# w_down: the column groups back and forth over the chunks, stored sums copied into the banks of a group's last run, low parts by DMA in two runs

## The chip, the cores and the metric

The kernel runs on one core of a Trainium2 chip. The time is that of the device for one execution, in microseconds; the median of several executions counts.

## The reference

One layer of an encoder with 512 tokens, a model width of 2048 and a hidden width of 5632, in float32: a projection, two kinds of attention side by side, an output projection with residual, and a SwiGLU block, with a final norm. The change touches only the last product of the SwiGLU block.

```python
h = rmsnorm(x, ffn_norm_w[l])
x = x + (jax.nn.silu(h @ w_gate[l]) * (h @ w_up[l])) @ w_down[l]
return rmsnorm(x, final_norm_w)
```

## The kernel before

**Precision.** The matmuls take operands in a shorter format (fp32r), and every operand is split in two: a high part, the number cast to that format by ACT, and a low part, the rest, by a subtraction on DVE. A product is three matmuls: high by high, high by low, low by high.

**Seven products in place of eight.** In the gate and up products and in `w_down`, the work is done in blocks of two by two, with seven products of sums of blocks in place of eight. `Blocks` holds what both share. An item is one load of weights `raw` (512 KB, R), a tile `S` of sums made from it (`sums`: three instructions of DVE, L1130 to L1132), and the splits (`split`: two casts of ACT, L1142, 128x768 for R and 128x1024 for S; and two subtractions of DVE, L1147). Every tile of that size lies in one of the slots `b` (s4); results and operands of 128x512 lie in the slots `a` (s2). A slot goes back to the end of the list of free ones when the last instruction that uses it is written, and the next `get` takes it from the front; with a kind given, it takes the first free slot that was used for that kind last. A slot's next writer waits until its last reader has ended. `most` is the number of raw loads that may be ahead.

**w_down.** Four jobs do k-tiles 0 to 3 and add their result to the residual in DRAM (`xd`). Then `Down.run` does the k-tiles 4 to 35, which are 16 pairs q = 2 to 17 of k-tiles, for each of four column groups c of 512 columns: 64 items. An item is 42 matmuls of 128x256 (`products`, L1539 to L1541), seven products of six, one PSUM bank for each of the seven. The pairs are cut in three chunks X (2 to 7), Y (8 to 12) and Z (13 to 17), and the order is chunk by chunk, in a chunk column group by column group, so there are 12 runs over the same c. At the end of each run the seven banks are copied out by ACT (`evac`, L1556 and L1558): four right after their products, three ("late") behind the splits of the next item. They go to `md` in DRAM, plain on SP's queue in the first chunk, adding on POOL's queue (GpSimd's DMAs) in the other two. After a group's last run `combine` reads its seven sums back (L1579), forms the four result tiles on DVE (L1590, L1591) and adds them, scaled, to the residual (L1604). It is a generator in `urgent`, of which one step is taken after each item.

**The operands.** For each q, `operands` makes four activation tiles and splits them (DVE L1488 to L1491, ACT L1500 and L1503, DVE L1501 and L1504), from `gd` in DRAM. `make(1)` takes one of the three steps of a q, after the products, where c is 3 or the item's number is odd; and as many as are missing when an item's q is not made yet. A q's slots are given back in c = 3.

**Around it.** The program writes instructions in the order of the Python code; each engine executes its own in that order, and waits are set by the tiles. After `Down` come the jobs for k-tiles 36 to 39 ("later", L303 to L305 and the splits L201, L202), then the last four k-tiles, the residual (L1419) and the final norm. An item's loop is in `run`: load, sums of up to two items ahead, splits of this and the next item, late evacuations, operands, products, one step of `urgent`.

## Time and profile before

| | |
|---|---|
| median of 3 executions | 2208.02 us (2207.67 to 2209.81) |
| the profiled execution | 2210.67 us, span 2208.9 us |
| mean granted TensorE clock | 0.997 |
| `Down` (64 items) | 1773.67 to 2106.80 us of the span |
| behind it, up to the last k-tiles | 2106.80 to 2166.00 us |
| last k-tiles and final norm | 2166.00 to 2208.90 us |

PE is TensorE's matmuls, PEld its weight loads, DVE VectorE, ACT ScalarE, POOL GpSimd, SP the engine that issues most DMAs. In the code, `R` and `S` are `b` slots, `pu` are PSUM banks in this stage. PEclk is the granted clock, 1.00 the full one. In the rows of waits, the first name is the engine, tile and line that waited, the second what ended the wait. In a timeline, the first two numbers are the start and the time of a row, and the bracket holds the idle time ahead of it and what ended it.

### The profile page before, as it was taken

Reading aid. Unit: us, or ns where it says so; the run is one execution under the profiler, and the core shown is the slowest. Engines: PE = TensorE matmul, PEld = TensorE weight load, DVE = VectorE, ACT = ScalarE, POOL = GpSimd, SP = SyncE. Lnnn points to the kernel's source line nnn. Section 1 sums busy time; section 2 is a strip of 40 time slices with the busy share of each in tenths; the row PEclk is TensorE's granted clock in tenths of the full one; section 3 lists DMA queues with packets and bytes.
Section 4 is the critical chain, followed back from the end, with each engine's and each line's share of the span. In section 5 each row is a group of like instructions: output and inputs, shape, how many; then the busy total and the mean of one; then the engine's idle time right before and its main releaser. Section 6 shows DMA issues by size and latency. Waiting matters only on the chain.

```text
span 2208.9 us, 33105 instructions
## 1 busy us (share of the span) xinstructions
PE 2185.1 (99%) x12374; PEld 1909.9 (86%) x12374; DVE 1564.8 (71%) x2720; ACT 1189.8 (54%) x1990; POOL 326.3 (15%) x349
## 2 busy tenths in 40 slices
PE   9999999999999999999999999999999999999998
PEld 7888888888888888888888888888888899999976
DVE  4366665754455346888888888888888897878777
ACT  5344444444445346666666666666666655555442
POOL 0000000000000011222222222222222200122220
PEclk9999999999999999999999999999999999999999
DMA  6525625241324434888888888888989865687892
GB/s 208 160 72 151 176 83 141 84 134 58 96 67 166 139 105 113 193 193 204 204 206 201 201 207 193 208 204 196 211 194 215 247 185 182 184 190 187 225 364 77
DMA packets 260273, 376.75 MB, mean 171 GB/s; under 512 B 18287, under 2 KB 179743, under 8 KB 260112
## 3 DMA queue, kind: packets, MB, share of 16 engines
q1 hardware_dynamic: 192800, 259.37, 37.3%
q0 software_dynamic: 66128, 114.21, 27.6%
q8 instruction: 97, 1.59, 0.3%
q10 hardware_dynamic: 1184, 1.06, 0.1%
q14 instruction: 64, 0.52, 0.1%
HBM read 246.58 MB, written 46.20 MB: 133 GB/s over the span
## 4 chain that ended last, share of the span: by engine, by line
PE 90%; DVE 4%; DMA 4%; ACT 1%; issue 1%; SPq 0%; ACTq 0%; DVEq 0%
PE pd L1275 22%; PE pd L1281 11%; PE ps L303 5%; PE ps L305 5%; PE ps L304 5%; PE ps L295 5%; PE ps L297 5%; PE ps L296 5%; PE pe L1275 4%; PE pu L1541 3%; PE pu L1540 3%; PE pu L1539 3%; PE pe L1281 2%; DMA b<-in_w_down_dram 2%; PE ps L529 1%; DVE b L1147 1%
## 5 line engine op out<-in xcount | busy, mean ns | idle before, releaser
L1275 PE MATMUL pd<-a,b 128*128 128x512 f32 x2112 | 528.4, 392 | 0.1
L1275 PEld LDWEIGHTS pd<-a,b 128*128 128x128 f32 x2112 | 378.9, 188 | 66.3 <-DVE a L1036 0.5
L1281 PEld LDWEIGHTS pd<-a,b 128*128 128x128 f32 x2112 | 288.5, 190 | 21.6
L1281 PE MATMUL pd<-a,b 128*128 128x256 f32 x2112 | 294.9, 282 | 0.0
L202 DVE TENSOR_TENSOR a<-b,a 128x512 fp32r<-128x512 f32 x288 | 192.9, 686 | 137.6 <-ACT a L201 136.2
L1182 POOL DMA_DIRECT2D b<-b x176 | 209.8, 1248 | 521.7 <-ACT b L1181 393.7
L1220 ACT CAST b<-b 128x1024 fp32r<-128x1024 f32 x176 | 185.4, 1053 | 166.6 <-DVE b L1206 138.4
L1541 PE MATMUL pu<-b,a 128*128 128x256 f32 x896 | 255.4, 285 | 6.4 <-DVE a L1504 5.4
L1540 PE MATMUL pu<-b,a 128*128 128x256 f32 x896 | 254.9, 285 | 0.0
L1539 PE MATMUL pu<-b,a 128*128 128x256 f32 x896 | 254.9, 284 | 0.0
L1221 DVE TENSOR_TENSOR b<-b,b 128x1024 fp32r<-128x1024 f32 x176 | 214.8, 1221 | 50.7 <-ACT b L1220 26.3
L201 ACT CAST a<-b 128x512 fp32r<-128x512 f32 x288 | 169.7, 617 | 68.1 <-PE ps L305 22.3
L1541 PEld LDWEIGHTS pu<-b,a 128*128 128x128 f32 x896 | 173.4, 194 | 7.2 <-DVE a L1504 6.1
L1539 PEld LDWEIGHTS pu<-b,a 128*128 128x128 f32 x896 | 173.5, 194 | 0.0
L1540 PEld LDWEIGHTS pu<-b,a 128*128 128x128 f32 x896 | 173.4, 194 | 0.0
L1142 ACT CAST b<-b 128x768 fp32r<-128x768 f32 (+1 forms) x128 | 115.2, 946 | 86.2 <-PE pu L1541 31.0
L1303 DVE TENSOR_TENSOR a<-pd,a 128x512 f32<-128x512 f32 x132 | 91.4, 692 | 96.5 <-ACT a L1302 96.5
L1181 ACT ACTIVATE b<-b 128x768 fp32r<-128x768 f32 x176 | 149.2, 847 | 4.7 <-PE ps L305 2.9
L1147 DVE TENSOR_TENSOR b<-b,b 128x768 fp32r<-128x768 f32 (+1 forms) x128 | 134.5, 1086 | 22.0 <-ACT b L1142 21.9
L1183 ACT CAST b<-b 128x768 fp32r<-128x768 f32 x176 | 145.2, 825 | 0.6 <-PE ps L305 0.6
L1302 ACT COPY a<-pd 128x512 f32<-128x512 f32 x132 | 77.5, 587 | 103.2 <-PE pd L1281 103.2
L1203 DVE TENSOR_TENSOR b<-b 128x512 f32<-128x512 f32 x176 | 120.3, 684 | 0.0
(246 smaller groups left out, 4328.8 us busy)
## 6 DMA issues: line engine op xcount, KB each, us to landing
b<-b POOLq DMA_DIRECT2D x176, 384.0 KB, 5.3
b<-in_w_gate_dram SPq DMA_DIRECT2D x88, 512.0 KB, 4.0
b<-in_w_up_dram SPq DMA_DIRECT2D x88, 512.0 KB, 4.5
b<-in_w_down_dram SPq DMA_DIRECT2D x88, 512.0 KB, 5.5
b<-in_w_in_dram SPq DMA_DIRECT2D x48, 512.0 KB, 4.0
b<-in_w_in_dram SPq DMA_DIRECT2D x94, 256.0 KB, 4.3
b<-in_w_out_dram SPq DMA_DIRECT2D x32, 512.0 KB, 4.7
md<-a POOLq DMA_DIRECT2D x56, 256.0 KB, 8.1
```

The costliest lines, as they stand in the source:

```text
L201: act.copy(h[2].t, r)
L202: dve.tensor_tensor(h[3].t, r, h[2].f, op=OP.subtract)
L1147: dve.tensor_tensor(lo.t, src, hi.f, op=OP.subtract)
L1181: act.activation(lo.t, r, AF.Copy, scale=-1.0)
L1182: pool.dma_start(out=lo.f, in_=r, accum_op=OP.add)
L1220: act.copy(hi.t, self.S[i].t)
L1221: dve.tensor_tensor(lo.t, self.S[i].t, hi.f, op=OP.subtract)
L1275: mm(o, wh.t[:, p, k], x_.t.rearrange("p s t -> p (s t)"), start=first and p == 0, stop=False, skip_group_check=True)
L1281: mm(o[:, 256:512], wl.t[:, p, k], x_.t[:, 0], start=False, stop=last and p == 1, skip_group_check=True)
L1539: mm(o, xh[:, t], wh, start=first and h == 0, stop=False, skip_group_check=True)
L1540: mm(o, xh[:, t], wl, start=False, stop=False, skip_group_check=True)
L1541: mm(o, xl[:, t], wh, start=False, stop=last, skip_group_check=True)
```

## The change

- **Order.** Ten runs in place of 12: groups 0, 1, 2 over X, group 3 over X and Y, groups 2 and 1 over Y, group 0 over Y and Z, groups 1, 2 and 3 over Z. They are numbered 0 to 9 here. The first six evacuate all seven banks at once, on POOL's queue.
- **Stored sums into banks.** Runs 6 to 9 are a group's last. One item ahead of such a run its seven sums are fetched from `md` (`fetch`), and in the last item of the run before, ACT copies them into the banks that come free (`preload`, L1564), in turn with the evacuations (L1609) or with the combine. The run then adds its products to them.
- **Combine from the banks.** In the last item of runs 6 to 9, `combine(c, n, bank)` follows each product: ACT copies two banks (L1627, L1635), DVE does seven operations (L1621, L1622, L1638), and the residual's four (L1652) come in two steps of `urgent`.
- **Low parts by DMA.** In runs 3 and 6 (21 items) the low part of R is made by an activation of ACT with scale −1 (L1481) and an adding DMA on POOL's queue (L1482) in place of DVE's subtraction.
- **Slots and operands.** `S`, splits and parts name a kind of slot; `most` goes from 3 to 4; `make` stands ahead of the products, takes one step more in runs 3 and 6, and keeps more slots back in runs 4 and 5.

```diff
-                S = self.S[i] = s4.get(F32, self.shape(4))
+                S = self.S[i] = s4.get(F32, self.shape(4), "sum")
...
-                    hi = s4.get(F32R, shape)
+                    hi = s4.get(F32R, shape, "split")
...
+                self.runs = [(0, X), (1, X), (2, X), (3, X + Y), (2, Y), (1, Y), (0, Y + Z), (1, Z), (2, Z), (3, Z)]
+                self.reserve = self.most = 4
...
+            def summed(self, r):
+                return r >= 6
+
+            def by_dma(self, i):
+                return i < self.n and self.seq[i][0] in (3, 6)
+
+            def part(self, i):
+                if not self.by_dma(i) or i in self.parts or i in self.sets:
+                    return
+                if i not in self.raw:
+                    self.load()
+                r = self.raw[i].t[:, :, 1:4]
+                hi, lo = (s4.get(F32R, self.shape(3), "part") for _ in range(2))
+                act.activation(lo.t, r, AF.Copy, scale=-1.0)
+                pool.dma_start(out=lo.f, in_=r, accum_op=OP.add)
+                act.copy(hi.t, r)
+                self.parts[i] = (hi, lo)
...
-                    if not raws or len(s2.free) < 9 + 4:
+                    if not raws or len(s2.free) < 9 + self.reserve:
...
+            def fetch(self, r):
+                c = self.runs[r][0]
+                for n in range(7):
+                    self.m[n] = s2.get()
+                    sp.dma_start(out=self.m[n].t, in_=md[7 * c + n])
+
+            def preload(self, n):
+                b = ps.get()
+                act.copy(b.t, self.m[n].t)
+                put(self.m.pop(n))
+                self.pre.append(b)
...
+                if ahead:
+                    self.preload(0)
...
-                        mm(o, xh[:, t], wh, start=first and h == 0, stop=False, skip_group_check=True)
+                        mm(o, xh[:, t], wh, start=first and not loaded and h == 0, stop=False, skip_group_check=True)
...
                     if last:
-                        if n < 4:
-                            self.evac(ch, c, n, self.banks[n])
+                        if loaded:
+                            self.combine(c, n, self.banks[n])
                         else:
-                            self.late.append((ch, c, n, self.banks[n]))
+                            self.evac(c, n, self.banks[n])
+                        if ahead and n < 6:
+                            self.preload(n + 1)
...
+                if n == 0:
+                    self.v, self.y = s2.get(), []
+                    act.copy(self.v.t, bank.t)
+                elif n == 1:
+                    self.y.append(s4.get(F32, [P, 2, 512]))
+                    add(self.y[0].t[:, :, up], M, halves(self.v))
+                elif n == 2:
+                    sub(self.v.t, self.v.t, bank.t)
+                elif n == 3:
+                    self.m4, self.w = s2.get(), s2.get()
+                    act.copy(self.m4.t, bank.t)
+                    add(self.w.t, self.m4.t, self.v.t)
+                elif n == 4:
+                    dve.scalar_tensor_tensor(self.v.t, bank.t, -1.0, self.v.t, op0=OP.mult, op1=OP.subtract)
+                elif n == 5:
+                    self.y.append(s4.get(F32, [P, 2, 512]))
+                    add(self.y[1].t[:, :, up], M, halves(self.w))
+                    sub(self.y[1].t[:, :, lo], halves(self.v), halves(self.m4))
+                    put(self.w, self.m4)
+                else:
+                    sub(self.y[0].t[:, :, lo], halves(self.v), M)
+                    put(self.v)
+                    urgent.append(self.residuals(c, self.y))
+                put(bank)
...
                     self.split(i + 1)
-                    self.evac_late()
+                    self.part(i + 2)
+                    self.reserve = 11 if r in (4, 5) else 4
                     while q not in self.x:
+                        self.reserve = 0
                         self.make(1)
+                    self.make((r in (3, 6)) + i % 2)
+                    if n == len(part) - 2 and r + 1 < len(self.runs) and self.summed(r + 1):
+                        self.fetch(r + 1)
...
                     self.products(i)
-                    if c == 3 or i % 2:
-                        self.make(1)
```

**The order at three places.** A name such as b12_1565 is slot b12 and a number that counts the tiles; the row says the output first, then what is read.

ACT, the casts for items 31 to 34, which lie within a run in both orders. Before (rows of the operands between the second and the third pair are left out; the raw tile is read first, then S):

```order
L1142 CAST b12_1565_18857<-b15_1548_18610 128x768
L1142 CAST b18_1566_18859<-b5_1557_18768 128x1024
L1142 CAST b10_1571_18913<-b6_1556_18702 128x768
L1142 CAST b1_1572_18915<-b9_1564_18853 128x1024
...
L1142 CAST b2_1577_18973<-b13_1562_18780 128x768
L1142 CAST b4_1578_18975<-b11_1570_18909 128x1024
L1142 CAST b12_1583_19029<-b15_1569_18865 128x768
L1142 CAST b19_1584_19031<-b5_1576_18969 128x1024
```

And after the change:

```order
L1142 CAST b3_1566_18846<-b1_1545_18574 128x768
L1142 CAST b12_1567_18848<-b17_1559_18779 128x1024
L1142 CAST b4_1572_18902<-b13_1551_18635 128x768
L1142 CAST b0_1573_18904<-b18_1565_18842 128x1024
L1142 CAST b3_1578_18958<-b15_1558_18710 128x768
L1142 CAST b5_1579_18960<-b17_1571_18898 128x1024
L1142 CAST b4_1584_19014<-b6_1564_18791 128x768
L1142 CAST b2_1585_19016<-b18_1577_18954 128x1024
```

The output slots of the casts of R were b12, b10, b2, b12, and are now b3, b4, b3, b4.

DVE, the operands of q = 11 and 12, whose first items are 27 and 28. Before: the subtraction of item 28's splits, q = 11's last four rows, then item 29's subtraction (L1147) and q = 12's last two behind the left-out rows:

```order
L1147 TENSOR_TENSOR b19_1547_18608<-b10_1537_18542,b18_1545_18604 128x1024
L1501 SCALAR_TENSOR_TENSOR a0_1348_18612<-b17_1499_18143,a0_1348_18612 128x256
L1504 TENSOR_TENSOR a58_1350_18614<-b17_1499_18143,a35_1349_18613 128x512
L1504 TENSOR_TENSOR a20_1352_18616<-a43_1346_18536,a4_1351_18615 128x512
L1504 TENSOR_TENSOR a46_1354_18618<-a37_1347_18537,a61_1353_18617 128x512
...
L1147 TENSOR_TENSOR b17_1555_18700<-b14_1543_18598,b1_1553_18696 128x1024
L1504 TENSOR_TENSOR a33_1361_18681<-a19_1355_18629,a32_1360_18680 128x512
L1504 TENSOR_TENSOR a52_1363_18683<-a24_1356_18630,a12_1362_18682 128x512
```

After the change: the subtraction for item 25 (L1494 is L1147's place for items with a low part by DMA), the last two rows of q = 11, the subtractions for items 26 and 27, and the last two of q = 12:

```order
L1494 TENSOR_TENSOR b4_1531_18434<-b17_1522_18353,b12_1530_18433 128x1024
L1538 TENSOR_TENSOR a31_1345_18378<-a15_1339_18368,a18_1344_18377 128x512
L1538 TENSOR_TENSOR a46_1347_18380<-a51_1340_18369,a43_1346_18379 128x512
...
L1494 TENSOR_TENSOR b3_1537_18495<-b18_1529_18429,b2_1536_18494 128x1024
...
L1494 TENSOR_TENSOR b12_1544_18571<-b17_1535_18490,b5_1543_18570 128x1024
L1538 TENSOR_TENSOR a20_1354_18515<-a42_1348_18505,a4_1353_18514 128x512
L1538 TENSOR_TENSOR a24_1356_18517<-a37_1349_18506,a61_1355_18516 128x512
```

q = 11 was finished behind item 28's subtraction and is now finished behind item 25's; q = 12 was finished behind item 29's and is now finished behind item 27's.

DVE, the combine. Before: the first steps of a group's combine, one step of two operations to an item (the rows that are left out are two of the sums):

```order
L1147 TENSOR_TENSOR b3_1713_20443<-b15_1697_20258,b4_1711_20439 128x768
L1147 TENSOR_TENSOR b18_1714_20445<-b10_1704_20362,b0_1712_20441 128x1024
L1590 TENSOR_TENSOR b12_1716_20507<-a53_1445_20178,a46_1444_20177 128x2x256
L1591 TENSOR_TENSOR a57_1446_20179<-a46_1444_20177,a57_1446_20179 128x512
L1130 TENSOR_TENSOR b19_1718_20511<-b13_1709_20374 128x512
...
L1147 TENSOR_TENSOR b14_1721_20519<-b6_1703_20316,b11_1719_20515 128x768
L1147 TENSOR_TENSOR b7_1722_20521<-b8_1710_20435,b9_1720_20517 128x1024
L1591 TENSOR_TENSOR a13_1448_20181<-a13_1448_20181,a57_1446_20179 128x512
L1590 TENSOR_TENSOR a57_1446_20179<-a54_1447_20180,a57_1446_20179 128x512
```

After the change: the last item of run 6, with the subtractions of the next item, the seven operations of the combine, two residuals, and then the next sums:

```order
L1147 TENSOR_TENSOR b5_1678_20055<-b15_1656_19793,b3_1676_20051 128x768
L1147 TENSOR_TENSOR b9_1679_20057<-b17_1671_19981,b12_1677_20053 128x1024
L1621 TENSOR_TENSOR b2_1681_20079<-pu3_60_19363,a18_1441_20069 128x2x256
L1622 TENSOR_TENSOR a18_1441_20069<-a18_1441_20069,pu4_61_19374 128x512
L1621 TENSOR_TENSOR a43_1443_20099<-a31_1442_20098,a18_1441_20069 128x512
L1638 SCALAR_TENSOR_TENSOR a18_1441_20069<-pu6_63_19396,a18_1441_20069 128x512
L1621 TENSOR_TENSOR b10_1682_20119<-pu7_64_19407,a43_1443_20099 128x2x256
L1622 TENSOR_TENSOR b10_1682_20119<-a18_1441_20069,a31_1442_20098 128x2x256
L1622 TENSOR_TENSOR b2_1681_20079<-a18_1441_20069,pu0_65_19418 128x2x256
L1652 SCALAR_TENSOR_TENSOR a37_1403_19524<-b2_1681_20079,small_76,a37_1403_19524 128x512
L1652 SCALAR_TENSOR_TENSOR a1_1404_19525<-b2_1681_20079,small_76,a1_1404_19525 128x512
L1130 TENSOR_TENSOR b17_1683_20133<-b1_1668_19928 128x512
```

The operations of a combine stood in pairs between the work of one item and the next, and now all seven and two residuals stand between the subtractions of one item and the sums ahead of those of the next.

More of the change, by code (lines that the diff above doesn't have):

```diff
@@ L1451, in layer, with __init__ @@
         class Down(Blocks):
-            def __init__(self, chunks):
-                self.chunks = chunks
-                self.begin([(ch, c, q) for ch in range(len(chunks)) for c in range(4) for q in chunks[ch]], 1, 256)
-                self.x = {}
-                self.making = self.operands()
-                self.late = []
-            def source(self, ch, c, q):
-                return w_down, 2 * q, 2, c * 512, 512
+            def __init__(self, X, Y, Z):
+                self.runs = [(0, X), (1, X), (2, X), (3, X + Y), (2, Y), (1, Y), (0, Y + Z), (1, Z), (2, Z), (3, Z)]
+                self.pairs = X + Y + Z
+                self.drop = {q: r for r, part in ((3, X), (6, Y), (9, Z)) for q in part}
+                self.begin([(r, q) for r, (c, part) in enumerate(self.runs) for q in part], 1, 256)
+                self.x, self.parts, self.m, self.pre, self.seen = {}, {}, {}, [], set()
+                self.reserve = self.most = 4
+                self.making = self.operands()
@@ new lines, in source @@
+            def source(self, r, q):
+                return w_down, 2 * q, 2, self.runs[r][0] * 512, 512
+            def summed(self, r):
[13 more added lines that the diff above has]
+                self.parts[i] = (hi, lo)
@@ new lines, in split @@
+            def split(self, i):
+                if not self.by_dma(i):
+                    return super().split(i)
+                if i in self.sets:
+                    return
+                self.part(i)
+                hi, lo = (s4.get(F32R, self.shape(4), "split") for _ in range(2))
+                act.copy(hi.t, self.S[i].t)
+                dve.tensor_tensor(lo.t, self.S[i].t, hi.f, op=OP.subtract)
+                self.sets[i] = [self.parts.pop(i), (hi, lo)]
+                put(self.raw.pop(i), self.S.pop(i))
+                self.load()
@@ L1525, in products @@
                 Z = lambda n: (sh.t[:, 0, n], sl.t[:, 0, n])
-                first, last = q == self.chunks[ch][0], q == self.chunks[ch][-1]
+                first, last = q == part[0], q == part[-1]
+                ahead = last and r + 1 < len(self.runs) and self.summed(r + 1)
                 if first:
-                    self.banks = []
+                    self.banks, self.pre = self.pre, []
+                loaded = self.summed(r)
+                if ahead:
+                    self.preload(0)
                 x_ = self.x[q]
@@ L1532, in products @@
                 for n, ((wh, wl), x) in enumerate(prods):
-                    if first:
+                    if first and not loaded:
                         self.banks.append(ps.get())
@@ L1559, in evac @@
                 put(bank)
[L1560 removed]
+                if (c, n) in self.seen:
                     pool.dma_start(out=md[7 * c + n], in_=y.t, accum_op=OP.add)
                 else:
[L1563 removed]
+                    pool.dma_start(out=md[7 * c + n], in_=y.t)
+                self.seen.add((c, n))
                 put(y)
[L1566 to L1571 removed]
@@ L1573, in combine @@
[L1573 to L1588 removed]
+            def combine(self, c, n, bank):
@@ L1610, in run @@
             def run(self):
-                for i, (ch, c, q) in enumerate(self.seq):
+                for i, (r, q) in enumerate(self.seq):
+                    c, part = self.runs[r]
+                    n = part.index(q)
                     self.load()
```

64 lines of the change are left out of this document (16 added, 48 removed).

## The prediction

> **What bounds the kernel now.** I read the first page for shares, then busy times by stage for w_down, then what TensorE waited for, then single rows round each gap.
>
> ```profile
> span 2208.9 us, 33105 instructions
> PE 2185.1 (99%) x12374; PEld 1909.9 (86%) x12374; DVE 1564.8 (71%) x2720; ACT 1189.8 (54%) x1990; POOL 326.3 (15%) x349
> ```
>
> TensorE is the bound. The change leaves its matmuls alone, so only TensorE's gaps and its clock can move the time. By stage (us, then busy time of PE, PEld, DVE, ACT, POOL, then PEclk, DMA share, GB/s):
>
> ```profile
> 1773.67:1909.74 136.07, 136.07 (x1135) 136.07 (x1134) 112.24 (x174) 75.67 (x109) 2.72 (x4) 1.00 0.59 185
> 1909.74:1924.94 15.20, 12.34 (x87) 11.73 (x85) 14.91 (x27) 7.60 (x12) 3.69 (x5) 0.89 0.74 186
> 1924.94:2020.69 95.75, 95.75 (x800) 95.75 (x799) 78.30 (x125) 54.70 (x80) 20.84 (x24) 1.00 0.80 190
> 2020.69:2031.04 10.35, 6.78 (x45) 6.58 (x44) 8.45 (x14) 5.16 (x9) 3.47 (x5) 0.84 0.73 123
> 2031.04:2106.80 75.76, 75.76 (x633) 75.76 (x632) 54.06 (x78) 36.76 (x52) 20.50 (x27) 1.00 0.91 249
> 2106.80:2166.00 59.20, 55.58 (x237) 43.75 (x237) 51.21 (x82) 22.03 (x38) 11.42 (x20) 1.00 0.82 283
> 2166.00:2208.90 42.90, 33.60 (x149) 27.37 (x147) 29.04 (x62) 14.19 (x42) 0.00 (x0) 0.95 0.27 98
> ```
>
> Rows 1, 3 and 5 hold 27, 19 and 15 items of `Down` without a gap: 136.07 / 27 = 95.75 / 19 = 5.04 us an item, 0.12 us a matmul. Rows 2 and 4 hold items 27, 28 and 48: 25.55 us where three items take 15.13, so **10.4 us** are lost there. What ended TensorE's waits (sum, count, longest), in `Down` and behind it:
>
> ```profile
> PE pu L1541 <- DVE a L1504: 5.4, 2, 3.6
> PE pu L1541 <- DVE a L1501: 0.9, 1, 0.9
> ...
> PE pu L303 <- DVE a L1419: 1.6, 1, 1.6
> PE pu L1720 <- DVE b L202: 1.0, 2, 0.9
> ```
>
> In `Down` it is the operands of q = 11, 12 and 17, which `make` finishes only when their first item is due (L1501, L1504). The other 4.1 us, 10.4 less 6.3, are half clock and shorter steps:
>
> ```profile
> 1919.99 0.39 PE L1541 MATMUL pu<-b,a 128*128 128x256 f32 x1 [1.83 <-DVE a L1504]
> 2026.10 0.38 PE L1541 MATMUL pu<-b,a 128*128 128x256 f32 x1 [3.57 <-DVE a L1504]
> 2142.93 0.47 PE L303 MATMUL pu<-a,a 128*128 128x512 f32 x1 [1.64 <-DVE a L1419]
> ...
> 1917.71:1921.12 3.41, 1.57 (x13) 1.37 (x13) 3.38 (x7) 1.05 (x3) 1.75 (x2) 1.00 0.73 162
> 1921.12:1924.53 3.41, 3.41 (x18) 3.41 (x18) 3.26 (x6) 3.11 (x6) 1.72 (x2) 0.50 1.05 180
> 2139.56:2142.97 3.41, 1.77 (x9) 1.18 (x7) 3.41 (x7) 2.42 (x6) 0.26 (x1) 1.00 1.04 411
> 2142.97:2146.38 3.41, 3.41 (x15) 2.85 (x16) 3.41 (x6) 2.70 (x5) 0.00 (x0) 1.00 1.05 409
> ```
>
> The first window has a gap of 1.83 us and the 3.41 us behind it run at clock 0.50, which costs about 3.41 / 2, less what falls on waits: 1.5 us. A gap of 1.64 us left the next window at 1.00. So here the line lies between 1.64 and 1.83 us.
>
> **The change part by part.**
>
> *Operand waits.* In the new order q = 12's operands are finished two items before item 28 and q = 17's two before item 48; nothing is forced there. The 10.4 us go: **−10.4** (bounds −10.4 and, if half the clock loss comes back elsewhere, −8.4).
>
> *Lead of the splits.* Before, the casts of an item stand two items ahead of it:
>
> ```profile
> 1940.30 1.79 ACT L1142 CAST b<-b 128x768 fp32r<-128x768 f32 x2 [3.25 <-PE pu L1541]
> 1946.01 2.75 ACT L1558 COPY a<-pu 128x512 f32<-128x512 f32 x4 [3.93 <-PE pu L1541]
> 1896.35 1.07 ACT L1558 COPY a<-pu 128x512 f32<-128x512 f32 x2
> ```
>
> The row at 1940.30 is the cast of item 34, which starts at 1950.13 (1924.94 + 5 x 5.04): 9.8 us ahead. In the new order the kind "split" hands the same two sets of slots back and forth (b3, b4, b3, b4 in place of b12, b10, b2, b12), and a set is free only when the item two earlier has ended. So a cast can start 4.8 us ahead, not 9.8. In a plain item that costs nothing: cast and subtraction of both parts end within 3.2 us. At the run ends, where other work stands ahead of the casts, the cover is gone. The rates:
>
> ```profile
> L1142 ACT CAST b<-b 128x1024 fp32r<-128x1024 f32 x63 | 66.3, 1052 | 5.0 <-DVE b L1132 5.0
> L1142 ACT CAST b<-b 128x768 fp32r<-128x768 f32 x63 | 52.9, 840 | 81.1 <-PE pu L1541 31.0 <-issue 23.7 <-PE pu L1540 16.0
> L1147 DVE TENSOR_TENSOR b<-b,b 128x1024 fp32r<-128x1024 f32 x63 | 76.8, 1219 | 0.0
> L1147 DVE TENSOR_TENSOR b<-b,b 128x768 fp32r<-128x768 f32 x63 | 60.0, 952 | 22.0 <-ACT b L1142 21.9
> L1558 ACT COPY a<-pu 128x512 f32<-128x512 f32 x72 | 41.4, 590 | 52.3 <-PE pu L1541 47.9
> 2057.72 0.68 DVE L1590 TENSOR_TENSOR b<-a,a 128x512 f32<-128x512 f32 x1
> 2058.32 0.68 DVE L1591 TENSOR_TENSOR a<-a,a 128x512 f32<-128x512 f32 x1
> 2058.92 0.68 DVE L1130 TENSOR_TENSOR b<-b 128x512 f32<-128x512 f32 x1
> ...
> 2060.44 2.08 DVE L1147 TENSOR_TENSOR b<-b,b 128x768 fp32r<-128x768 f32 x2
> 2079.50 1.41 DVE L1604 SCALAR_TENSOR_TENSOR a<-b,small,a 128x512 f32<-128x512 f32 x2
> ```
>
> So a 128x512 operation of DVE takes 0.60 us from start to start, the three sums 1.52 (2058.92 to 2060.44), both subtractions about 2.1, two residuals 1.4; ACT copies a bank in about 0.6. A bank as the source of DVE isn't in these rows for TENSOR_TENSOR; I take 0.60, and 0.70 as the upper bound.
>
> *Run ends 0 to 4.* Seven evacuations at once in place of four and three: ACT has 7 x 0.59 = 4.1 us of copies in an item of 5.04 us and casts 0.5 us later. That is under the 1.6 us left (4.8 less 3.2), so **0** (0 to +2).
>
> *Run end 5 to 6.* ACT alternates seven preloads and seven evacuations, each waiting for the bank that the other frees: some 1.0 to 1.15 us a pair, so ACT comes free at T + 9.5 to 10.5 (T: TensorE's start of the run's last item). Queued behind are the cast of the sums for the item that starts at T + 10.1 and the low part of the item after. I reckon 1.2 us of stall for each and take **+2.5** (bounds 1.5 and 4).
>
> *Run ends 6 to 7, 7 to 8, 8 to 9.* This is the dear part. DVE has the next item's subtractions until T + 3.2. Then the combine, interleaved with ACT's copies, since a preload needs the bank that a combine step frees: two steps end at T + 4.4, ACT's third and fourth preloads and the copy of M4 at T + 5.6, then five DVE steps end at T + 8.75. Two residuals (1.4) and three sums (1.5) stand ahead of the subtraction for the item that starts at T + 10.1, and that (0.95) ends at T + 12.7. TensorE needs it at T + 10.2: a stall of 2.5 us. At 6 to 7 the order starts earlier and I get 1.8. Together **+7.0**. From below: if the combine's DVE steps ran as early as the banks are done (the last at T + 5.04, one step to T + 5.7), the subtraction would end at T + 9.6 and nothing stall: 0. From above, with 0.70 for each of seven steps: 3 x 0.7 more, 9.
>
> *Clock.* Two of those gaps, 2.5 us, lie above the 1.83 that halved the clock, though the gap must also lie well in a window. At 0.7 each, 2 x 0.7 x 1.5 = **+2.1** (0 to 4.5). The Trainium skill, "TensorE: Matmul & The Clock Gate", in its rules for kernels, asks only that gaps stay under about 3 us, and puts the half clock behind a whole idle window; by it gaps of 2.5 us cost no clock and the sum would be 2.1 lower. The rows above show a halved window behind 1.83 us, so I go by them.
>
> *Low parts by DMA in runs 3 and 6.* 21 subtractions of 128x768 (0.95 us) leave DVE, which has slack there; 21 activations join ACT, and 21 accumulating transfers of 384 KB POOL's queue. An earlier stage shows this operation:
>
> ```profile
> L1182 POOL DMA_DIRECT2D b<-b x176 | 209.8, 1248 | 521.7 <-ACT b L1181 393.7
> b<-b POOLq DMA_DIRECT2D x176, 384.0 KB, 5.3
> 900.00:1700.00 800.00, 800.00 (x4592) 705.00 (x4591) 657.76 (x1066) 510.43 (x699) 206.75 (x184) 1.00 0.88 202
> b<-b POOLq DMA_DIRECT2D x13, 384.0 KB, 5.6
> q0 software_dynamic: 3824, 6.16, 56.6%
> ```
>
> It lands 5.3 us after issue, at a DMA share of 0.88. The last two rows are 60 us of that stage: 13 transfers take at most 56.6% of the 16 engines, about 2.4 us each, 48% of an item. On top of 0.59 (first row of the table by stage) that is 1.07: the DMA engines would be full in these 21 items. The source is written at T_i + 2.05 and TensorE needs the result at T_i + 10.2, so 8.1 us are to be had against 5.3. I take a few late ones: **+1.5** (0 to 6). The Trainium skill, "DMA: Bandwidth & Descriptors", section on the anatomy of a DMA from GpSimd, fits 2.0 us plus bytes at 436 KB a us, by my estimate 2.9 us for 384 KB; by that no low part is late and the sum is 1.5 lower. The measured 5.3 decides.
>
> *Fewer transfers through DRAM.* 42 partial sums go out on POOL's queue where 84 went on two, 28 come back as before. SP loses plain writes and keeps the raw loads ahead. Hidden by the raw loads' lead: 0.
>
> *The tail.* Behind `Down`, 59.20 us hold 3.62 us of gaps, and ACT and DVE clear old business:
>
> ```profile
> L1604 DVE SCALAR_TENSOR_TENSOR a<-b,small,a 128x512 f32<-128x512 f32 x12 | 8.6, 747 | 1.7 <-DMA a<-xd 1.5
> ACT a L201 <- DMA md<-a: 12.5, 2, 9.1
> ```
>
> 12 of the 16 residuals lie here, three of four combines, some 7 x 0.6 + 4 x 0.7 = 7 us of DVE each, with 51.21 of 59.20 us busy. In the new order all four combines are done in `Down`, the last residuals excepted. But the last combine then stands ahead of the splits of the later jobs, and I leave a stall of 1.3 us at their start (two residuals, 1.4, at that place). 3.62 less 1.3: **−2.3** (−3.6 to 0).
>
> Sum: −10.4 + 0 + 2.5 + 7.0 + 2.1 + 1.5 − 2.3 = +0.4 us. The profiled execution took 2210.67 (span 2208.9 and 1.8 around it), 2.65 above the median of the runs, 2208.02. Carried to the median, 0.4 is less than any term is known to, and I forecast no change: **2208.0**.
>
> **The rivals.** A measurement of this kernel can tell about 0.2% (4.4 us) from no change: under 2203.6 is faster, over 2212.4 slower.
>
> *Faster: DVE gets through the combine in time.* For it: the lower bound of the run-end term is 0, and TensorE's earlier stalls push casts ahead of their need. Against it: the written order puts residuals and sums ahead of the subtraction, and before, at 2055 to 2062, just two such steps were put between items. If half of the 7.0 is real, the gaps stay under 1.64, the clock holds and low parts land: −10.4 + 2.5 + 3.5 − 3.6 = −8.0, so 2200. It decides from the point at which the combine's last step ends before T + 7.5. Floor: 2208.0 − 10.4 − 3.6 = 2194.0.
>
> *Slower: the low parts land late.* The one mechanism: DMA at a share over 1 in runs 3 and 6, so that transfers queue. It decides from a landing time of 8.1 us, a median against 5.3 now and 2.9 if unloaded (my reckoning from 2.4 us of engine time and a start). At 8.6 us each of 21 items is 0.5 late, 10.5 us in place of 1.5, 9 more: 2217. For it speaks the sum 0.59 + 0.48; against it that 0.88 with the same transfers ran 800 us without a gap, and that raw loads have four buffers here and may fall back.
>
> *The waits don't go.* Operands late elsewhere, for example in runs 4 and 5, where a reserve of 11 slots holds `make` back: −10.4 becomes 0 and the rest stays, 2218.4. The order speaks against it: q = 13 to 17 are done by two items before need.
>
> **How the numbers follow.** No change within 0.2%: 0.42. Faster: 0.31. Slower through the low parts 0.16, through run ends at their upper bounds (9 + 4 + 4.5 against the 11.6 of the sum, 2214) 0.08, through waits that stay 0.03: 0.27. The range goes from just under the faster rival to the slower one: 2199 to 2217, with about one in ten beyond either end. The likeliest case's own range is 2203.6 to 2212.4.
>
> **What the changed profile would show.** Items 27, 28 and 48 at 5.04 us, and no wait of TensorE for operand splits (right: the first term). At the ends of runs 6, 7 and 8 a TensorE wait of 1.8 to 2.5 us for the subtraction of the raw weights' low part, one item after the run's last, with DVE busy throughout; without it the run-end term is wrong. A window at clock 0.50 behind one or two of these. Waits for the low parts' DMA in runs 3 and 6 not over 2 us in all; if they add up to 5 or more the slower rival holds. Behind `Down` one gap of some 1.3 us and few others. The forecast fails above all if DVE's combine is shorter or longer at the run ends than my chain by hand, since three of them hang on it.

## The result, and the profile after

The changed kernel takes **2225.78 us** (median of 6 executions, 2224.24 to 2228.13), the kernel before 2208.98 beside it: a ratio of 1.0077, 95% interval 1.0064 to 1.0090. It is 16.8 us slower, outside the range of 2199 to 2217. The profiled execution has a span of 2222.5 us, 13.6 over that of the one shown before; the one before was 1.7 us above its median, the one after 1.5 below its own, which is why the traces differ by 3 us less than the medians.

The changed kernel's page, and its time by stage (busy time of PE, PEld, DVE, ACT, POOL, then PEclk, DMA share, GB/s):

```profile
span 2222.5 us, 33130 instructions
PE 2186.6 (98%) x12374; PEld 1912.7 (86%) x12374; DVE 1554.6 (70%) x2699; ACT 1201.8 (54%) x2005; POOL 322.5 (15%) x356
...
1881.32:1972.04 90.72, 90.72 (x758) 90.72 (x757) 72.04 (x114) 53.44 (x77) 17.25 (x23) 1.00 0.80 216
1972.04:2000.28 28.24, 18.03 (x128) 17.01 (x127) 14.24 (x27) 16.93 (x27) 10.41 (x14) 0.88 1.08 278
2000.28:2035.56 35.28, 35.28 (x296) 35.28 (x295) 26.82 (x46) 21.09 (x31) 6.46 (x9) 1.00 0.88 245
2035.56:2051.04 15.48, 12.08 (x87) 11.67 (x85) 14.00 (x21) 6.83 (x10) 2.16 (x4) 0.89 0.48 156
2071.20:2080.98 9.78, 6.77 (x44) 6.57 (x43) 9.61 (x15) 2.31 (x3) 0.92 (x2) 0.83 0.56 166
2101.14:2109.49 8.35, 5.30 (x44) 5.10 (x43) 8.21 (x14) 2.35 (x3) 1.74 (x4) 1.00 0.47 146
2124.77:2169.95 45.18, 44.15 (x194) 35.91 (x193) 37.12 (x59) 19.93 (x37) 0.00 (x0) 1.00 0.26 89
```

The first row shown of the stages is 18 items at 5.04 us (21 to 38), with items 27 and 28 among them: the operand waits are gone, and item 48 lies in the third. The second is items 39 to 41, run end 5 to 6: 28.24 us for 15.12, so **13.1** lost, at a DMA share of 1.08 (called full below). The rows of 15.48 (items 49 and 50, less 10.08), 9.78 and 8.35 (items 55 and 60, less 5.04 each) are the three later run ends: 5.4 + 4.7 + 3.3 = **13.4** lost. What ended TensorE's waits in `Down` and right behind it:

```profile
PE pu L1592 <- DVE b L1147: 9.3, 3, 3.2
PE pu L1592 <- DMA b<-b: 9.1, 3, 5.7
PE pu L1591 <- ACT pu L1564: 2.5, 3, 1.2
PE pu L304 <- DVE a L202: 0.9, 1, 0.9
```

L1147 is the subtraction for R at the three later run ends; `b<-b` are the accumulating transfers that make a low part (items 20, 39 and 41); L1564 is the preload.

### The profile page after: what moved, and what is told of

The parts are those of the page before. It is cut to its first block, busy times and chain, and to the rows that moved or that the text cites. A ratio compares the mean times of both kernels' runs of the same rounds, so it can differ in the third digit from the quotient of the medians.

```text
span 2222.5 us, 33130 instructions
## 1 busy us (share of the span) xinstructions
PE 2186.6 (98%) x12374; PEld 1912.7 (86%) x12374; DVE 1554.6 (70%) x2699; ACT 1201.8 (54%) x2005; POOL 322.5 (15%) x356
## 4 chain that ended last, share of the span: by engine, by line
PE 92%; DMA 2%; DVE 2%; issue 2%; ACT 1%; POOL 0%; SPq 0%; ACTq 0%; POOLq 0%; DVEq 0%
PE pd L1275 22%; PE pd L1281 11%; PE ps L303 5%; PE ps L304 5%; PE ps L305 5%; PE ps L295 5%; PE ps L297 5%; PE ps L296 5%; PE pe L1275 4%; PE pu L1592 3%; PE pu L1593 3%; PE pu L1591 3%; PE pe L1281 2%; PE ps L529 1%; PE pu L304 1%
## 5 line engine op out<-in xcount | busy, mean ns | idle before, releaser
L202 DVE TENSOR_TENSOR a<-b,a 128x512 fp32r<-128x512 f32 x288 | 192.7, 687 | 130.9 <-ACT a L201 130.6
L1183 ACT CAST b<-b 128x768 fp32r<-128x768 f32 x176 | 145.5, 827 | 0.6 <-PE ps L305 0.6
L1142 ACT CAST b<-b 128x768 fp32r<-128x768 f32 x86 | 77.0, 941 | 108.9 <-PE pu L1593 104.6
L593 ACT CAST b<-ps 128x512 fp32r<-128x512 f32 x64 | 37.6, 587 | 144.8 <-PE ps L529 142.9
```

The source lines that it names most:

```text
L202: dve.tensor_tensor(h[3].t, r, h[2].f, op=OP.subtract)
L1183: act.copy(hi.t, r)
```

## The experiments

Two questions: why run end 5 to 6 costs 13.1 us where 2.5 was forecast, and what the 3-us stall at the others is made of. Times are medians, with the kernel before measured beside experiments 1 to 10 (2209.1 to 2209.6).

**1. Low parts on DVE again.**

```diff
-                return i < self.n and self.seq[i][0] in (3, 6)
+                return False
```

> The changed kernel with the low parts of runs 3 and 6 made by DVE again (no accumulating DMA, 21 subtractions of 0.95 us more, 21 activations fewer). Theory A, too many transfers at once at run end 5 to 6: TensorE's 9.1 us of waits for low parts go, and so do most of its 2.5 us of waits for preloads, since the fetched sums land sooner; with the clock's share about 12 of the 13.1 us lost at items 39 to 41 and the 1.5 of item 20: 2212 to 2216 where the change has 2225.8. Rival B, ACT's row of seven preloads and seven evacuations holds the casts back whatever DMA does: item 41 then waits for DVE's subtraction in place of the DMA, some 5 us stay: 2218 to 2221. The three later run ends stay at 3.2 us of wait each under both.

2217.64 us, ratio to before 1.0038 (1.0023 to 1.0053): 8 us off the change, between the two forecasts. Items 39 to 41 lose 3.0 us in place of 13.1, and that is theory A's side. What comes for it lies in items 42 to 49, where DVE has two steps of `make` in the odd items of run 6 and the subtractions back: items 43, 45 and 47 lose 0.6 us each, and items 48 and 49, which wait for preloads, 2.6. Item 60 loses 1.5 more, by a half-clock window that it didn't have in the change.

**2. Fetch two items earlier.**

```diff
-                    if n == len(part) - 2 and r + 1 < len(self.runs) and self.summed(r + 1):
+                    if n == len(part) - 4 and r + 1 < len(self.runs) and self.summed(r + 1):
```

> The changed kernel with the seven stored sums fetched two items earlier (four items from the end of the run in place of two). Theory A: ACT no longer waits for the fetched sums (4.3 us in all at run end 5 to 6), its activation for item 41 comes 4 us earlier, TensorE's wait of 5.7 us there falls to 1 to 2 and the 2.5 us for preloads to under 1: 2217 to 2221. Rival B: the fetch was in time anyway, the alternation sets the pace: no change, 2224 to 2227. Run ends 6 to 8 as before the edit, 3.0 to 3.2 us.

2216.70 us, ratio 1.0035 (1.0022 to 1.0048), just under A's 2217 to 2221. ACT's copies at the end of run 5, of the change and then with this edit (idle time before the copies last):

```profile
L1564 ACT COPY pu<-a 128x512 f32<-128x512 f32 x7 | 4.1, 590 | 4.3 <-DMA a<-md 4.3
L1609 ACT COPY a<-pu 128x512 f32<-128x512 f32 x7 | 4.1, 580 | 0.0
...
L1564 ACT COPY pu<-a 128x512 f32<-128x512 f32 x7 | 4.1, 590 | 0.2
```

ACT no longer waits for the fetched sums, as A expected, and TensorE's waits for preloads fall from 2.5 to 0.3. But item 41's wait didn't fall to 1 to 2; it rose from 5.7 to 6.7: its transfer is issued 4.5 us earlier, TensorE is there 4.5 us earlier too, and it still lands 10.8 us after issue. Theory A had the wrong cause for that wait. Most of the gain, 6.2 of 7.6 us between the two traces, came from where nothing was expected: the three later run ends wait 1.2, 2.6 and 2.6 in place of 3.2, 3.0 and 3.0, and no window there is at half clock.

**3. Slots without kinds.**

```diff
-                    hi = s4.get(F32R, shape, "split")
+                    hi = s4.get(F32R, shape)
...
```

(likewise for `lo`, sums and parts)

> The changed kernel without kinds for the slots of sums, splits and parts in this stage, so that casts can start two items ahead again. Theory C, the lost lead: DVE has the next item's subtractions done before a run's last item starts, the combine follows TensorE's products and ends near T + 6, and the three waits of 3.0 to 3.2 us for L1147 at items 50, 55 and 60 fall under 0.7 with both half-clock windows: some 11 us less, 2213 to 2216. Rival D, the combine's place in the order ahead of the subtraction is enough by itself: the waits stay at 2.5 us or more, 2223 to 2226. Run end 5 to 6 unchanged under both, within 3 us.

2217.56 us, ratio 1.0038 (1.0023 to 1.0053). In time it lies between C and D, and only 1.5 us of the gain between the traces are at the three run ends; 2.8 are at items 39 to 41 and 1.5 at item 20. The waits are 2.9, 1.4 and 2.6. DVE round the last item of run 7 of this kernel (T = 2055.77; start, time; in the bracket the idle time before and what ended it) shows why:

```profile
2054.47 1.22 DVE L1147 TENSOR_TENSOR b<-b,b 128x1024 fp32r<-128x1024 f32 x1
2057.68 0.69 DVE L1621 TENSOR_TENSOR b<-pu,a 128x512 f32<-128x512 f32 x1 [1.99 <-ACT a L1627]
2058.48 0.69 DVE L1622 TENSOR_TENSOR a<-a,pu 128x512 f32<-128x512 f32 x1
2060.33 0.69 DVE L1621 TENSOR_TENSOR a<-a,a 128x512 f32<-128x512 f32 x1 [1.17 <-ACT a L1635]
2061.14 0.69 DVE L1638 SCALAR_TENSOR_TENSOR a<-pu,a 128x512 f32<-128x512 f32 x1
```

DVE is free at T, where the change had T + 3.2, as C said. But it idles 2 us there: the first preload on ACT waits for the fetched sums, and the copy L1627 stands behind it:

```profile
2056.54 0.59 ACT L1564 COPY pu<-a 128x512 f32<-128x512 f32 x1 [4.56 <-DMA a<-md]
2057.07 0.58 ACT L1627 COPY a<-pu 128x512 f32<-128x512 f32 x1
```

The lead alone isn't enough; the fetch is late next.

**4. The three together.**

> The three edits together: low parts on DVE, fetch two items earlier, no kinds. Theories A and C: operand waits gone and run ends nearly free, 2225.8 less 1.5, 12 and 11: 2199 to 2204, faster than the kernel before (2209.0). Rivals B and D: 2216 to 2221.

2207.12 us, ratio 0.9991 (0.9981 to 1.0000): the same as before, 3 us short of A and C. Items 55 and 60 wait 1.2 us in place of 3.0 and without half clock; item 50 still waits 3.2. There DVE comes without a pause out of the odd items of run 6 and reaches the combine only at T + 4.2.

**5. Item 41's low part ahead of the copies.**

```diff
                     self.part(i + 2)
+                    if r == 5 and n == len(part) - 1:
+                        self.part(i + 3)
```

> The changed kernel with one edit: the activation, the accumulating transfer and the cast of R for item 41 are written ahead of the row of preloads and evacuations in item 38, not behind it. Theory A2, the low part of item 41 is late because its activation stands behind 14 copies on ACT (it ran at T38 + 15.7 us in the change, at T38 + 11.2 with the early fetch) and its transfer then takes about 10 us behind seven evacuations on the same queue: TensorE's wait of 5.7 us at item 41 goes wholly, and 1 us of clock with it; the waits for preloads (2.5) and at item 39 (2.1) stay or grow by up to 1: 2217 to 2220 where the change has 2225.8. Rival B2, the DMA engines are full from 1964 to 2000 us and whatever is early makes something else late: the waits at items 39 to 41 still sum to 9 us or more, 2223 to 2226.

2223.02 us, ratio 1.0064 (1.0049 to 1.0079), within rival B2's 2223 to 2226. Item 41's wait went wholly, as A2 said, but item 42 now waits 2.8 us for its own transfer, and item 39 waits 2.8 in place of 2.1. Items 39 to 42 lose 11.9 us in all, where they lost 13.1; their waits are 6.8 us, though, not the 9 that B2 named. With the engines full, what is put ahead makes something else late.

**6. Residuals one item later.**

```diff
-                    run_urgent()
+                    if not (self.summed(r) and n == len(part) - 1):
+                        run_urgent()
```

> The changed kernel with the two residuals behind a combine taken one item later, behind the next subtractions of DVE (1.4 us leave the chain between the combine and the subtraction that TensorE waits for). Theory C2, that chain on DVE sets the end: each of the three waits of 3.0 to 3.2 us falls by 1.3 to 1.5 and the half-clock windows behind items 50 and 55 (1.6 us each) go: 4.2 + 3.2, so 2217 to 2220. Rival D2, DVE isn't what ends it (ACT's casts of the same item, behind its preloads, are): the waits fall by less than 0.5, 2223 to 2226.

2219.36 us, ratio 1.0047 (1.0032 to 1.0062), as C2 expected: the three waits are 1.8, 1.8 and 1.6, though only one of the two half-clock windows went. The first stall behind `Down` (L304, 0.9 us) goes too; the later jobs take 43.74 us in place of 45.18.

**7. The operands' schedule alone, on the kernel before.**

```diff
                     if c == 3 or i % 2:
-                        self.make(1)
+                        self.make(2 if c == 3 else 1)
```

> The kernel before with one edit: make takes two steps in place of one in the items of c = 3, so that q = 11, 12 and 17 are finished five items or more ahead. Theory A (the first term of the prediction, alone): the 10.4 us at items 27, 28 and 48 go, with the half clock, and nothing comes for them; the tail stays: 2209.0 less 10, 2198 to 2200. Rival: DVE has up to 3 us more in the items of c = 3 and gets late there or at a run end: 2202 to 2209, with TensorE's waits for L1147 in items 18 to 24 and 39 to 44.

2204.30 us, ratio 0.9979 (0.9969 to 0.9988): **4.9 us faster** by the medians, not 10. All of `Down` before, and with this edit, in its fastest execution:

```profile
1773.67:2106.80 333.13, 326.70 (x2690) 325.89 (x2689) 267.97 (x413) 179.90 (x259) 51.22 (x63) 0.99 0.73 199
...
1773.50:2099.28 325.78, 323.88 (x2690) 322.97 (x2689) 267.77 (x413) 180.56 (x259) 51.33 (x63) 1.00 0.74 204
```

```profile
PE pu L1540 <- DVE b L1147: 1.9, 4, 0.6
```

Items 27, 28 and 48 take 5.04 us, but 3.0 of the 10.4 come back, as the rival said: in and right behind the items of c = 3 (items 24, 25 and 42 to 44) DVE now has two steps of `make`, and its subtractions come 0.4 to 0.6 us late, with the slower steps around the gap 0.6 to 0.9 us at each of four items.

**8. Four edits to the change** (2, 3, 5 and 6; low parts stay on DMA).

> The changed kernel with low parts by DMA kept, and four edits: no kinds, fetch two items earlier, item 41's low part ahead of the copies, residuals one item later. By A2 and C2 run end 5 to 6 loses under 2 us and the three later ones under 1 each: 2209.0 less 10.4 and 4.4, plus 0.3 and about 3: 2196 to 2200. By B2 and D2 5 to 9 us more: 2202 to 2208.

2204.01 us, ratio 0.9978 (0.9969 to 0.9987): run ends 6 to 8 wait 0, 0.7 and 0.7 us, as expected, but item 42 waits 4.1 us for its low part. B2 holds for run end 5 to 6, C2 for the others.

**9. The low parts of items 39 to 43 on DVE** (edits 2, 3 and 6, and by DMA only run 3 and items 44 to 48).

```diff
-                return i < self.n and self.seq[i][0] in (3, 6)
+                return i < self.n and (self.seq[i][0] == 3 or self.seq[i][0] == 6 and self.seq[i][1] >= 13)
```

> The four-edit kernel with one difference: the low parts of items 39 to 43 are made by DVE, and only run 3 and items 44 to 48 keep the accumulating transfers (so item 41's need not be moved). Theory E, the DMA engines are full (share 1.04 to 1.10 from 1970 to 2000 us) because the low parts fall on the seven evacuations of run 5, and a transfer that takes 5.3 us elsewhere takes 10: without these five, item 42's wait of 4.1 us and its half-clock window go, DVE's extra 0.95 us an item costs about 1: 2204.0 less 7 plus 1, 2197 to 2200. Rival F, the evacuations, the reads of xd and the raw loads fill the engines by themselves: item 41 or 42 then waits for its weights or for x operands instead, 2202 to 2206.

**2198.96 us** (2198.85 to 2200.75), ratio 0.9954 (0.9941 to 0.9968): 10.6 us faster than before, 26.8 than the change, and as theory E expected, not rival F. 1970 to 2000 us of the change, and of this kernel:

```profile
1970.00:2000.00 30.00, 19.79 (x143) 18.77 (x142) 15.09 (x30) 18.71 (x30) 11.02 (x15) 0.89 1.08 277
...
1970.00:2000.00 30.00, 28.97 (x240) 28.56 (x239) 23.78 (x42) 22.56 (x35) 8.87 (x13) 1.00 0.97 234
```

What still waits in it:

```profile
PE pu L1592 <- DVE b L1147: 2.4, 4, 0.7
PE pu L1592 <- DMA b<-b: 1.1, 1, 1.1
```

All of `Down` in this kernel:

```profile
1775.03:2102.74 327.71, 324.20 (x2690) 323.03 (x2689) 269.30 (x423) 192.37 (x271) 54.81 (x82) 1.00 0.75 219
```

That is no less than the 325.78 of experiment 7 (326.96 when repeated, experiment 12). What this kernel has over the one-line schedule lies behind `Down`: 96.3 us in place of 101.1.

**10. Run 5 without its seven accumulating transfers.**

```diff
-                if (c, n) in self.seen:
+                if (c, n) in self.seen and c == 1:
+                    pass
+                elif (c, n) in self.seen:
```

> The changed kernel without the seven accumulating transfers at the end of run 5 (the sums of run 5 are not added to the stored ones of column group 1; ACT's copies stay). Theory E: item 41's transfer is issued at the same place on ACT but lands in 5 to 6 us in place of 9.75, and TensorE's wait there falls from 5.7 to 1 to 2 us, with its clock: span 2222.5 less 5, about 2217. Rival, the place behind ACT's copies by itself: landing stays at 9 us or more, the wait at 5 or more, span 2221 to 2224.

The result then lacks run 5's part of the sums of column group 1. 2218.93 us in one execution, span 2217.2, where theory E had about 2217. Item 41's transfer, issued at 1983.84 in the change and at 1983.17 here:

```profile
b<-b POOLq DMA_DIRECT2D x1, 384.0 KB, 9.8
...
b<-b POOLq DMA_DIRECT2D x1, 384.0 KB, 3.8
```

Same place on ACT, same queue, and 3.8 us in place of 9.8; TensorE doesn't wait for it any more. So the evacuations in flight made it late, not its place behind ACT's copies. They held up more than their own queue: the two raw loads that SP issues beside them took 10.1 and 10.8 us in the change and 5.3 and 4.4 here. How much of the 9.8 us was the order in POOL's queue, where four evacuations were still ahead, and how much the full engines, these runs don't divide. Items 39 and 43 still wait 2.0 us each for their low parts.

**11 and 12. Second profiled executions**, of the kernel before and of experiment 7.

> The kernel before once more, for a second profiled execution. Theory G, the half-clock windows at items 28 and 48 (about 1.5 us each) depend on where the gap falls, so that the 10.4 us of the first term are 7.4 to 10.4 by execution and the median of the runs holds fewer of them: an execution with another time than 2210.67 shows one or none of the two windows at 0.50. Rival: both windows stand in every execution, and items 27, 28 and 48 lose 10.4 us again within 0.5; the executions then differ elsewhere.

> The kernel before with two steps of make in the items of c = 3, once more. Its first profiled execution was its fastest (2202.1 against a median of 2204.3). Theory H, executions of the same kernel differ ahead of w_down, where no edit of this study reaches: the stage of w_down takes 320 to 321 us again, and the rest carries the difference. Rival: the w_down stage itself is longer in this execution by 2 us or more, with a window at half clock.

Before, 2210.09 us: `Down` takes 332.98 us where it took 333.13, so on the sum the rival to G holds and the 10.4 us stand. But the half-clock windows moved. Item 28 in the execution shown first, and here:

```profile
1916.32:1924.94 8.62, 6.79 (x45) 6.58 (x43) 8.43 (x14) 5.00 (x8) 3.69 (x5) 0.80 0.77 146
...
1916.53:1923.66 7.13, 5.29 (x44) 5.09 (x43) 7.03 (x13) 3.72 (x6) 3.49 (x4) 1.00 0.67 140
...
1920.20 0.39 PE L1541 MATMUL pu<-b,a 128*128 128x256 f32 x1 [1.83 <-DVE a L1504]
```

The same gap of 1.83 us cost a half-clock window once and none the other time; item 48 lost 1.4 us more instead. Experiment 7 again, 2204.38 us: `Down` 326.96 in place of 325.78 (the 320 to 321 in the expectation was a wrong figure; the first execution had 325.8), and 1.1 us more ahead of it, where the edit doesn't reach. So neither H nor its rival alone holds. Why executions of the kernel before differ by up to 6 us (2205.3 to 2211.5) is left open.

## Why the prediction was wrong, step by step

| term | forecast | in the trace after |
|---|---|---|
| operand waits | −10.4 | −10.4 |
| run ends 0 to 4 | 0 | 0 |
| run end 5 to 6 | +2.5 | +13.1 |
| the three later run ends, with their clock | +7.0 + 2.1 | +13.4 |
| other low parts | +1.5 | +1.5 (item 20) |
| behind `Down` | −2.3 | −4.4 |
| ahead of `Down` | | +0.3 |
| sum | +0.4 | +13.5 (spans: +13.6) |

*The step that failed is run end 5 to 6*: 2.5 us forecast, 13.1 measured. The prediction put 1.2 us of stall on the cast for item 40 and 1.2 on the low part of item 41, both behind ACT's row of copies, and took the low part to land 5.3 us after its issue. Item 40 waited 0.2. Item 41's transfer was issued at 1983.84; with 5.3 us it would have landed at 1989.1, 1.2 us after TensorE wanted it. It took 9.8, and TensorE waited 5.66:

```profile
1993.63 0.58 PE L1592 MATMUL pu<-b,a 128*128 128x256 f32 x1 [5.66 <-DMA b<-b]
...
1990.24:1993.65 3.41, 0.02 (x1) 0.02 (x1) 3.34 (x8) 2.59 (x4) 0.89 (x1) 0.55 1.09 212
1993.65:1997.07 3.42, 3.42 (x16) 3.42 (x17) 3.15 (x7) 0.00 (x0) 0.00 (x0) 0.50 1.05 358
```

The half clock behind this wait (1990.56 to 1997.39) cost 1.9 us more, and the sum had a price for the clock only at the later ends. Two waits stood in no term of this run end: 2.1 us for item 39's low part and 2.3 for preloads. With item 40's 0.2 that is 12.1 of the 13.1; the rest is slower steps around the gaps.

The price of the landing came from a stage with a share of 0.88, and I set "fewer transfers through DRAM" to 0, as hidden by the lead of the raw loads. At this one place, seven reads of `md`, seven accumulating writes, the low parts, reads of `xd` and `gd` and the raw loads fall into 36 us (1964 to 2000). The prediction's own 1.07, in which the `md` traffic is only an average over its stage, should have warned of it. Experiments 9 and 10 show the cause from both sides, without the low parts and without the evacuations; 5 and 8 show that moving one transfer ahead doesn't remove it.

I also took the fetched sums to be there in time. ACT waited 4.3 us for them and ended its row at T + 14.9 (T = 1967.00, item 38), not at T + 9.5 to 10.5. That isn't what made item 41 late: with the early fetch (experiment 2) the row ended at T + 10.6, as forecast, and item 41 waited 6.7 us.

That the other low parts cost 1.5 us as forecast is luck: item 20 alone makes it, where I had a few of the 21 late. The waits for low parts add up to 9.1 us in all, over the 5 that the prediction named as the sign of its slower rival.

*The three later run ends* had the right place, engine and line, and 9.3 us of waits for the subtraction where I had 7.0 (its three stalls, 1.8 and twice 2.5, add up to 6.8). DVE at the end of run 7 (T = 2061.12, item 53):

```profile
2064.65 0.69 DVE L1621 TENSOR_TENSOR b<-pu,a 128x512 f32<-128x512 f32 x1 [0.28 <-ACT a L1627]
2065.44 0.69 DVE L1622 TENSOR_TENSOR a<-a,pu 128x512 f32<-128x512 f32 x1
2067.31 0.69 DVE L1621 TENSOR_TENSOR a<-a,a 128x512 f32<-128x512 f32 x1 [1.17 <-ACT a L1635]
2068.11 0.69 DVE L1638 SCALAR_TENSOR_TENSOR a<-pu,a 128x512 f32<-128x512 f32 x1
...
2069.91 0.68 DVE L1622 TENSOR_TENSOR b<-a,pu 128x512 f32<-128x512 f32 x1
2070.63 1.42 DVE L1652 SCALAR_TENSOR_TENSOR a<-b,small,a 128x512 f32<-128x512 f32 x2
...
2073.48 2.09 DVE L1147 TENSOR_TENSOR b<-b,b 128x768 fp32r<-128x768 f32 x2
```

The last step ended at T + 9.5, not T + 8.75: the first preload waits 0.4 us for the fetched sums (which holds L1627 back), and the steps come 0.6 to 0.8 us apart. What follows is as forecast: residuals, sums, the subtraction. The experiments divide the stall of about 3 us at items 55 and 60: the early fetch takes 0.4 us off (2), the lead of the slots another 1.4 (4 against 2; the low parts on DVE, which 4 also has, change nothing at these ends by themselves, as 1 shows), the later residuals alone 1.3 to 1.4 (6) and 0.5 on top of the others (9 against 4); 0.7 are left.

*The clock* cost 3.4 us at these ends, two ends of three, where the sum had 2.1. But the line I drew, between gaps of 1.64 and 1.83 us, is wrong: the length of a gap doesn't decide. In the change, item 60 waited longer than item 55 and went on at full clock (0.83 and 1.00 in the rows of 9.78 and 8.35 us):

```profile
2074.49 0.39 PE L1592 MATMUL pu<-b,a 128*128 128x256 f32 x1 [3.01 <-DVE b L1147]
2104.47 0.39 PE L1592 MATMUL pu<-b,a 128*128 128x256 f32 x1 [3.05 <-DVE b L1147]
```

What the traces show instead is a grid of windows. The half-clock windows of the change start at 1990.56, 2045.17 and 2075.89, 16 and 9 times 3.413 us apart. Cut on that grid, the gap of item 55 leaves TensorE idle for 2.01 us of one window, and the next is halved; that of item 60 is split, 1.78 and 1.27, and no window is:

```profile
2072.48:2075.89 3.41, 1.40 (x11) 1.40 (x12) 3.34 (x6) 1.04 (x1) 0.00 (x0) 1.00 0.69 216
2075.89:2079.31 3.42, 3.42 (x19) 3.42 (x18) 3.35 (x7) 0.00 (x0) 0.00 (x0) 0.50 0.42 141
2099.79:2103.20 3.41, 1.63 (x14) 1.43 (x12) 3.31 (x7) 2.66 (x4) 2.12 (x4) 1.00 0.81 267
2103.20:2106.61 3.41, 2.14 (x17) 2.14 (x18) 3.41 (x5) 1.05 (x1) 0.00 (x0) 1.00 0.73 245
```

In the 14 traces of this study, from 20 us after the start, every window at full clock with 1.91 us or more of TensorE idle was followed by one at half clock, none with 1.72 or less was, and of the eight between (1.75 to 1.90) two were. So a gap of 2 to 3 us costs 1.7 us or nothing by where it falls: all three later run ends were halved in experiment 1 and none in 2, and part of the difference between such profiles is this luck. The Trainium skill, "TensorE: Matmul & The Clock Gate", Part 1, says that the gate's window of 3.4 us runs free of the kernel; the grid agrees with that. The Trainium skill's advice there ("Why this matters for your kernels") to keep gaps under about 3 us doesn't protect here: 1.83 us was enough once in two.

*The operand waits* went as forecast, and by a schedule that the other parts aren't needed for: in one line, experiment 7 takes 6.0 to 7.4 us off `Down` in its two traces.

*The tail* gained more than forecast; I had counted the later jobs alone, but the last k-tiles and the final norm got shorter too. Before, both stages, and the last one after:

```profile
2106.80:2154.06 47.26, 44.73 (x192) 35.38 (x191) 39.31 (x63) 20.57 (x36) 11.42 (x20) 1.00 1.03 354
2154.06:2208.90 54.84, 44.45 (x193) 35.74 (x192) 40.94 (x81) 15.65 (x45) 0.00 (x0) 0.96 0.21 77
...
2169.95:2222.50 52.55, 43.52 (x192) 35.70 (x191) 27.83 (x60) 14.52 (x42) 0.00 (x0) 0.94 0.22 80
```

47.26 became 45.18 and 54.84 became 52.55. DVE's 40.94 us in the last stage became 27.83: some 5.6 us of it were residuals and steps of a combine, and the rest is splits and additions of the later jobs (L202, L1419), which now run earlier.

*The rivals.* The slower one named the right mechanism, DMA engines over their share, and the wrong extent: its point of decision was a median landing of 8.1 us, and over the 21 items of the change there stands (least, median, most)

```profile
DMA to landing us min/median/max: 4.3/7.0/10.4
```

so three items waited, not 21. Its 2217 were passed all the same, since the lateness sits in one place, where the evacuations meet the low parts, and brought waits for preloads and half clock with it. The faster rival failed at its own point: the combine ended at T + 9.5, not before T + 7.5.

## What to carry to other kernels

Price a transfer at the place where it will run: add up what else is in flight in those microseconds, since a landing time of 5.3 us, from a stage at a DMA share of 0.88, became 9.8 at 1.08, though the kernel moves fewer bytes in all (374.0 MB after 376.8). Where a change bundles a schedule with a new data path, try the schedule alone: one line on the old kernel gave 4.9 us of the 10.6 of the best kernel here, and the new path paid only after its fetch, its slots and its residuals were moved and five of its transfers given back to DVE, and then only behind the stage it was made for. Where such a path puts work ahead of the steps that feed the bounding engine, list everything that stands in that row on each engine; here a wait of 3 us was made of several pieces, and it fell to 0.7 only when three of them were moved.

## What the runs showed of the hardware

A 384-KB accumulating transfer took from 3.8 to 11.9 us from issue to landing in one and the same stage (experiments 10 and 3), by what was in flight. The half-clock windows lie on a grid of 3.413 us, and a window at full clock was followed by one at half clock when TensorE had been idle for 1.91 us or more of it, never at 1.72 or less. So the same gap of 1.83 us was followed by a half-clock window in one execution and not in the next, and longer ones, split between two windows, passed at full clock: 3.05 us in the change, and this one with the early fetch:

```profile
2068.86 0.38 PE L1592 MATMUL pu<-b,a 128*128 128x256 f32 x1 [2.63 <-DVE b L1147]
2065.96:2073.87 7.91, 5.28 (x44) 5.08 (x43) 7.77 (x13) 2.03 (x3) 0.53 (x2) 1.00 0.52 179
```
